# A two-layer decoder on one core: the low parts of unscaled weights are summed by an accumulating DMA in place of VectorE

## The chip, the cores and the metric

The kernel runs on 1 core of one Trainium2 chip. The metric is device microseconds of an execution. Three runs of the kernel before took 1812.57, 1816.09 and 1816.96 us; the median is 1816.09 us.

## The reference, cut to what matters

The input `x` is 512 tokens of 2048 values in float32. Two layers follow each other; each adds to the stream the normalised output of a mixer.

```
layer 0 (S5):   u, z = split(rmsnorm(h) @ w_in)          # 2048 x 4096
                y = gelu(state_space(u))                 # diagonal scan, 128 groups of 16 channels
                y = y * sigmoid(y @ w_glu + b_glu)       # 2048 x 2048
                h = h + rmsnorm((y * silu(z)) @ w_out)   # 2048 x 2048
shared:         k, v, f = split(rmsnorm(h) @ kv_w)       # 2048 x (2048 + 2048 + 16)
layer 1 (FoX):  q, z = split(rmsnorm(h) @ fox_w_in)      # 2048 x 4096
                o = causal attention of 16 heads with cumulative log forget gates
                h = h + rmsnorm((o * silu(z)) @ fox_w_out)
```

All products are wanted to about float32 precision.

## The kernel before

Every large product is made of three matmuls in the type float32r. Each operand is split into a high part, its copy in float32r, and a low part, the difference between the original and the high part. `mm3` (line 168) adds high times high, low weights times high, and high weights times low. So each piece of weights has a tile `whi` and a tile `wlo`, and both must be there before the matmuls on it can go on.

`piece` (line 138) prepares one piece, normally 128 partitions by 1024 elements (512 KB): it loads `wraw` from DRAM, multiplies it by a norm's scale where there is one, has ScalarE copy it to `whi` (through `act`, line 85), and has VectorE or GpSimd subtract to give `wlo` (line 152). `wraw` has four buffers, `whi` and `wlo` have two each. A column of 128 outputs needs two pieces; on each, TensorE runs 24 matmuls of 512 columns. `stream` and `ahead` keep one column prepared: after the matmuls of a column are issued in the program, the pieces of the next are asked for. The order of instructions on each engine is fixed when the program is built; the tile framework sets the semaphores.

The work runs in stages:

- Phase A: `w_in`, 32 columns (16 of `u`, 16 of `z`), with the state-space work between them: tables (`btps`), small kernels (`kps`), scans (`xps`) and outputs (`yps`), one of each for 16 steps. The first two columns are prepared by code of their own. The weights are unscaled. After the start, the queue that issues the weight loads (`self.weng`) is GpSimd's.
- Phase B: `w_glu`, 16 columns, unscaled, loads on GpSimd's queue.
- Phase C: `w_out`, by tokens (`tok_stage`, line 210), unscaled: 24 pieces of 512 output columns, then 8 of 256. The last two of these go to buffers of their own. Loads on SyncE's queue (SP), as in the stages that follow.
- Phase D: the columns of `k`, `q`, `v` and `z`, 128 pieces in all, each with a scale that GpSimd multiplies in (line 148), and the attention of 16 heads.
- Phase E: `fox_w_out`, as phase C.

Within `piece`, the instructions have a raised priority when `urgent` is set, so that they stand ahead of other work that is ready.

Of the kernel before, what the change touches and what calls it, by code (L numbers as in the profile page):

```python
# [12 lines left out]
F32R = mybir.dt.float32r  # L13
I32 = mybir.dt.int32
AF = mybir.ActivationFunctionType
ALU = mybir.AluOpType
# [49 lines left out]
class Kern:  # L66
# [72 lines left out]
    def piece(self, src, scale=None, pool=None, urgent=True, eng=None):  # L139

        nc = self.nc
        shp = list(src.shape)
        wp, n = pool or (self.wp, "")
        with self.tc.high_priority() if urgent else ExitStack():
            raw = self.wp.tile(shp, F32, tag="wraw", name="wraw", bufs=4)
            self.weng.dma_start(raw, src)
            if scale is not None:
                (eng or nc.vector).tensor_tensor(raw, raw, scale.unsqueeze(2).to_broadcast(shp), op=ALU.mult)  # L148
            hi = wp.tile(shp, F32R, tag=f"whi{n}", name="whi", bufs=2)
            lo = wp.tile(shp, F32R, tag=f"wlo{n}", name="wlo", bufs=2)  # L150
            self.act(hi, raw)
            (eng if eng and scale is None else nc.vector).tensor_tensor(lo, raw, hi, op=ALU.subtract)  # L152
        return hi, lo

    def stream(self, items, urgent=True):
# [975 lines left out]
```

## Time and profile before

| | |
|---|---|
| time of the three runs, median | 1816.09 us |
| the profiled execution: time | 1817.64 us |
| its span in the trace | 1815.9 us |
| mean granted clock of TensorE | 0.995 |
| TensorE matmul busy | 1786.6 us (98%) |
| VectorE busy | 1115.2 us (61%) |
| ScalarE busy | 614.4 us (34%) |
| GpSimd busy | 362.2 us (20%) |

The span is the stretch that the trace covers; the profiled execution's time lies 1.7 us above it. PE is TensorE's matmuls, PEld its weight loads, DVE VectorE, ACT ScalarE, POOL GpSimd, SP SyncE. Matmuls overlap in the engine, so a row that says 0.39 us for one does not mean that they follow each other at that distance; the starts tell that. Engine queues that only issue transfers have a q behind their name.

### The profile page before, as it was taken

Reading aid. Unit: us, or ns where it says so; the run is one execution under the profiler, and the core shown is the slowest. Engines: PE = TensorE matmul, PEld = TensorE weight load, DVE = VectorE, ACT = ScalarE, POOL = GpSimd, SP = SyncE. Lnnn points to the kernel's source line nnn. Section 1 sums busy time; section 2 is a strip of 40 time slices with the busy share of each in tenths; the row PEclk is TensorE's granted clock in tenths of the full one; section 3 lists DMA queues with packets and bytes.
Section 4 is the critical chain, followed back from the end, with each engine's and each line's share of the span. In section 5 each row is a group of like instructions: output and inputs, shape, how many; then the busy total and the mean of one; then the engine's idle time right before and its main releaser. Section 6 shows DMA issues by size and latency. Waiting matters only on the chain.

```text
span 1815.9 us, 26272 instructions
## 1 busy us (share of the span) xinstructions
PE 1786.6 (98%) x10518; PEld 1537.6 (85%) x10518; DVE 1115.2 (61%) x1629; ACT 614.4 (34%) x1032; POOL 362.2 (20%) x254
## 2 busy tenths in 40 slices
PE   9999999999999999999999999999999999999996
PEld 6888888888788888899889898989888898988886
DVE  9789999995855523256665655555555656542324
ACT  7334333333633322235223323222323332332222
POOL 1000000000000000033333433333333334300002
PEclk9999999999999999999999999999999999999998
DMA  9545555555544553343223323232232322344332
GB/s 326 144 137 157 146 149 147 145 147 168 186 146 153 165 186 93 94 134 128 82 88 93 94 89 94 86 99 87 88 99 87 97 90 88 93 134 162 93 95 103
DMA packets 141339, 226.57 MB, mean 125 GB/s; under 512 B 53601, under 2 KB 80497, under 8 KB 140961
## 3 DMA queue, kind: packets, MB, share of 16 engines
q1 hardware_dynamic: 126000, 173.79, 30.9%
q0 software_dynamic: 13056, 47.33, 8.7%
q10 hardware_dynamic: 2160, 3.77, 0.6%
q8 instruction: 82, 1.34, 0.3%
q14 instruction: 41, 0.33, 0.1%
HBM read 201.88 MB, written 22.97 MB: 124 GB/s over the span
## 4 chain that ended last, share of the span: by engine, by line
PE 90%; DVE 4%; DMA 2%; ACT 2%; SPq 1%; issue 1%; DVEq 0%; ACTq 0%
PE proj L171 18%; PE proj L173 18%; PE proj L172 17%; PE tok L232 6%; PE tok L233 6%; PE tok L231 6%; PE v L205 3%; PE v L206 3%; PE v L207 3%; PE yps L534 1%; DVE wlo L152 1%; PE t L940 1%; PE yps L539 1%; PE xps L506 1%; ACT ah L85 1%; PE btps L432 1%
## 5 line engine op out<-in xcount | busy, mean ns | idle before, releaser
L152 DVE TENSOR_TENSOR wlo<-wraw,whi 128x1024 fp32r<-128x1024 f32 x284 | 413.6, 1457 | 451.5 <-ACT whi L85 447.8
L85 ACT ACTIVATE whi<-wraw 128x1024 fp32r<-128x1024 f32 (+2 forms) x292 | 306.3, 1050 | 844.0 <-PE proj L173 518.5
L148 POOL TENSOR_TENSOR wraw<-wraw,vecs 128x1024 f32<-128x1024 f32 (+1 forms) x128 | 265.4, 2073 | 612.0 <-DMA wraw<-kv_k 281.5
L172 PE MATMUL proj<-BH,wlo 128*128 128x512 f32 (+1 forms) x816 | 308.9, 378 | 3.6 <-DVE wlo L152 3.6
L173 PE MATMUL proj<-BL,whi 128*128 128x512 f32 (+1 forms) x816 | 309.1, 379 | 1.9 <-DVE BL L73 1.9
L171 PE MATMUL proj<-BH,whi 128*128 128x512 f32 (+1 forms) x816 | 310.5, 380 | 0.0
L171 PE MATMUL proj<-ah,whi 128*128 128x512 f32 x768 | 302.5, 394 | 2.1 <-ACT zt L85 1.5
L173 PE MATMUL proj<-al,whi 128*128 128x512 f32 x768 | 300.3, 391 | 2.2 <-DVE al L73 1.7
L172 PE MATMUL proj<-ah,wlo 128*128 128x512 f32 x768 | 299.7, 390 | 0.2
L172 PEld LDWEIGHTS proj<-BH,wlo 128*128 128x128 f32 x816 | 154.6, 190 | 31.9 <-DVE wlo L152 4.1
L173 PEld LDWEIGHTS proj<-BL,whi 128*128 128x128 f32 x816 | 154.6, 189 | 30.7 <-DVE BL L73 2.3
L171 PEld LDWEIGHTS proj<-BH,whi 128*128 128x128 f32 x816 | 154.5, 189 | 27.8 <-ACT BH L85 0.2
L173 PEld LDWEIGHTS proj<-al,whi 128*128 128x128 f32 x768 | 144.1, 188 | 36.3 <-DVE al L73 6.3
L171 PEld LDWEIGHTS proj<-ah,whi 128*128 128x128 f32 x768 | 144.1, 188 | 33.6 <-ACT zt L85 1.9
L172 PEld LDWEIGHTS proj<-ah,wlo 128*128 128x128 f32 x768 | 144.2, 188 | 31.2 <-DVE wlo L152 1.3
L205 PE MATMUL v<-whi,BH 128*128 128x256 f32 (+1 forms) x512 | 145.6, 284 | 0.0
L206 PE MATMUL v<-wlo,BH 128*128 128x256 f32 (+1 forms) x512 | 145.2, 284 | 0.0
L207 PE MATMUL v<-whi,BL 128*128 128x256 f32 (+1 forms) x512 | 145.2, 284 | 0.0
L232 PE MATMUL tok<-wlo,BH 128*128 128x512 f32 (+1 forms) x320 | 111.0, 347 | 1.4 <-DVE wlo L152 1.4
L232 PE MATMUL tok<-wlo,ah 128*128 128x512 f32 (+1 forms) x320 | 111.0, 347 | 0.0
L231 PE MATMUL tok<-whi,BH 128*128 128x512 f32 (+1 forms) x320 | 110.9, 347 | 0.0
L233 PE MATMUL tok<-whi,al 128*128 128x512 f32 (+1 forms) x320 | 110.9, 347 | 0.0
(202 smaller groups left out, 2542.3 us busy)
## 6 DMA issues: line engine op xcount, KB each, us to landing
wraw<-w_fox SPq DMA_DIRECT2D x64, 512.0 KB
wraw<-w_in POOLq DMA_DIRECT2D x58, 512.0 KB, 4.4
wraw<-w_glu POOLq DMA_DIRECT2D x32, 512.0 KB, 4.3
wraw<-w_out SPq DMA_DIRECT2D x32, 512.0 KB
wraw<-kv_k SPq DMA_DIRECT2D x32, 512.0 KB
wraw<-w_fo SPq DMA_DIRECT2D x32, 512.0 KB
wraw<-kv_v SPq DMA_DIRECT2D x28, 512.0 KB
M<-kd SPq DMA_DIRECT2D x128, 64.0 KB
```

The source lines that it names most:

```text
L85: self.nc.scalar.activation(out, in_, f, **kw)
L148: (eng or nc.vector).tensor_tensor(raw, raw, scale.unsqueeze(2).to_broadcast(shp), op=ALU.mult)
L152: (eng if eng and scale is None else nc.vector).tensor_tensor(lo, raw, hi, op=ALU.subtract)
L171: mm(ps, lhsT=hi, rhs=xh, start=(k == 0), stop=False)
L172: mm(ps, lhsT=lo, rhs=xh, start=False, stop=False)
L173: mm(ps, lhsT=hi, rhs=xl, start=False, stop=(k == self.K - 1))
L205: nc.tensor.matmul(o, lhsT=xh[k][:, bs], rhs=hi, start=(k == 0), stop=False)
L206: nc.tensor.matmul(o, lhsT=xh[k][:, bs], rhs=lo, start=False, stop=False)
L207: nc.tensor.matmul(o, lhsT=xl[k][:, bs], rhs=hi, start=False, stop=(k == K - 1))
L231: nc.tensor.matmul(ps, lhsT=xh[k][:, bs], rhs=hi, start=(k == 0), stop=False)
L232: nc.tensor.matmul(ps, lhsT=xh[k][:, bs], rhs=lo, start=False, stop=False)
L233: nc.tensor.matmul(ps, lhsT=xl[k][:, bs], rhs=hi, start=False, stop=(k == K - 1))
```

## The change

For pieces without a scale, the subtraction is no longer made by VectorE or GpSimd. ScalarE writes the high part as before, then writes its negative into `wlo`; a transfer that GpSimd issues then adds `wraw` onto `wlo`, in SBUF. For pieces with a scale, the subtraction stays on VectorE.

```diff
             hi = wp.tile(shp, F32R, tag=f"whi{n}", name="whi", bufs=2)
-            lo = wp.tile(shp, F32R, tag=f"wlo{n}", name="wlo", bufs=2)
-            self.act(hi, raw)
-            (eng if eng and scale is None else nc.vector).tensor_tensor(lo, raw, hi, op=ALU.subtract)
+            if scale is None:
+
+                lo = wp.tile(shp, F32R, tag=f"wlo{n}", name="wlo", bufs=2)
+                self.act(hi, raw)
+                self.act(lo, hi, AF.Copy, scale=-1.0)
+                nc.gpsimd.dma_start(lo, raw, accum_op=ALU.add)
+            else:
+                lo = wp.tile(shp, F32R, tag=f"wlo{n}", name="wlo", bufs=2)
+                self.act(hi, raw)
+                nc.vector.tensor_tensor(lo, raw, hi, op=ALU.subtract)
         return hi, lo
```

## Rows read from the trace of the kernel before

**Rows 1.** Page, part 1: busy us, share of the span, instructions.

```profile
PE 1786.6 (98%) x10518; PEld 1537.6 (85%) x10518; DVE 1115.2 (61%) x1629; ACT 614.4 (34%) x1032; POOL 362.2 (20%) x254
```

**Rows 2.** Page, part 4: the chain that ended last, by engine.

```profile
PE 90%; DVE 4%; DMA 2%; ACT 2%; SPq 1%; issue 1%; DVEq 0%; ACTq 0%
```

**Rows 3.** TensorE's waits: waiter, awaited, us in total, times, longest us.

```profile
PE proj L172 <- DVE wlo L152: 3.6, 1, 3.6
...
PE tok L232 <- DVE wlo L152: 1.4, 1, 1.4
```

**Rows 4.** Timeline of ScalarE in phase C: start us, duration, what.

```profile
642.81 1.06 ACT L85 ACTIVATE whi<-wraw 128x1024 fp32r<-128x1024 f32 x1 [1.57 <-PE tok L233]
648.25 1.06 ACT L85 ACTIVATE whi<-wraw 128x1024 fp32r<-128x1024 f32 x1 [4.38 <-PE tok L233]
```

**Rows 5.** Timeline of VectorE in phase C.

```profile
643.90 1.22 DVE L152 TENSOR_TENSOR wlo<-wraw,whi 128x1024 fp32r<-128x1024 f32 x1 [1.94 <-ACT whi L85]
```

**Rows 6.** Timeline of phase B: two matmuls of TensorE, 24 apart.

```profile
599.72 0.39 PE L171 MATMUL proj<-ah,whi 128*128 128x512 f32 x1
...
605.16 0.39 PE L171 MATMUL proj<-ah,whi 128*128 128x512 f32 x1
```

**Rows 7.** DMA queues and issues (KB each, us to landing), and `wraw`'s landings.

```profile
q0 software_dynamic: 13056, 47.33, 8.7%
wraw<-w_in POOLq DMA_DIRECT2D x58, 512.0 KB, 4.4
wraw<-w_glu POOLq DMA_DIRECT2D x32, 512.0 KB, 4.3
mask<-c_mask POOLq DMA_DIRECT2D x1, 64.0 KB, 4.1
DMA to landing us min/median/max: 3.9/4.4/7.6
```

**Rows 8.** Timeline of VectorE and GpSimd in phase B.

```profile
504.24 1.22 DVE L152 TENSOR_TENSOR wlo<-wraw,whi 128x1024 fp32r<-128x1024 f32 x1
...
505.75 0.53 POOL L146 DMA_DIRECT2D wraw<-w_glu  x1 [6.68 <-DVE wlo L152]
```

**Rows 9.** The chain, in order of time: start us, us, what.

```profile
393.84 3.71 DMA y_d<-gy
```

**Rows 10.** The chain in phase A: state-space work between columns.

```profile
130.44 0.87 PE btps L432 x8
...
134.90 1.08 PE xps L506 x32
...
147.14 0.88 PE btps L432 x8
...
158.91 0.61 PE kps L472 x16
...
162.68 0.93 PE xps L506 x32
```

**Rows 11.** TensorE around one gap: timeline, then windows (PEclk is granted clock).

```profile
875.75 0.28 PE L171 MATMUL proj<-BH,whi 128*128 128x256 f32 x1
879.62 0.58 PE L172 MATMUL proj<-BH,wlo 128*128 128x256 f32 x1 [3.60 <-DVE wlo L152]
...
core 0: us, PE busy (x) PEld busy (x) DVE busy (x) ACT busy (x) POOL busy (x), PEclk, DMA share, GB/s
879.00:880.00 1.00, 0.38 (x1) 0.38 (x2) 1.00 (x2) 0.00 (x0) 0.00 (x0) 0.50 0.00 0
885.00:886.00 1.00, 1.00 (x9) 1.00 (x9) 0.00 (x0) 0.00 (x0) 0.24 (x1) 0.74 0.00 0
```

**Rows 12.** Windows inside phases A, B, C, E, columns as in rows 11.

```profile
100.00:400.00 300.00, 300.00 (x2387) 253.10 (x2389) 284.41 (x331) 112.33 (x192) 21.74 (x42) 1.00 0.54 147
430.00:635.00 205.00, 202.61 (x912) 164.45 (x911) 118.48 (x132) 84.02 (x104) 16.43 (x31) 1.00 0.53 168
640.00:800.00 160.00, 158.59 (x821) 136.40 (x820) 48.97 (x50) 41.91 (x65) 8.27 (x4) 1.00 0.38 120
1595.00:1795.00 200.00, 199.62 (x1097) 174.51 (x1096) 73.18 (x110) 55.98 (x92) 3.87 (x3) 1.00 0.36 114
```

## The prediction

> **What bounds the kernel now.** I read the page's busy shares and the chain first. TensorE (PE) is busy 98% of the span and carries 90% of the chain that ended last; VectorE carries 4% [rows 1, 2]. Then I asked what TensorE waits for: the longest single wait on a `wlo` of line 152 is 3.6 us, once, and it is on a scaled weight (the operand `BH` in `proj`), which the change does not touch; among unscaled weights it is 1.4 us, once [rows 3]. So the VectorE time that the change frees (156 subtractions of 1.22 us [rows 5], 190 us) comes from an engine that TensorE hardly waits for. At best it brings a microsecond or two. The question is whether the new path to `wlo` still meets its deadline.
>
> The deadline comes from the timeline. A piece of weights serves 24 matmuls, and TensorE takes 5.44 us over them (from 599.72 to 605.16 [rows 6]). `whi` and `wlo` have two buffers, so the copy to `whi` of a piece starts when TensorE leaves the piece two before it, and copies follow at the same 5.44 us [rows 4]. When the next copy starts, TensorE is already at this piece. A piece thus has 5.44 us from the start of its `whi` copy to the matmul that reads `wlo`, less some 0.2 us for the weight load ahead of it. Today the copy ends at 643.87 and VectorE's subtraction at 645.12 [rows 4, 5]: 2.3 us used, 2.9 to spare.
>
> **What the change removes, adds and moves.** There are 156 unscaled pieces: 60 of `w_in` (the first two columns do not pass through `piece`), 32 of `w_glu`, 32 each of `w_out` and `w_fo` (by the code: 24 full pieces and 8 of half width). The 128 scaled pieces keep their path, and I cost the whole attention stage at nothing.
>
> ScalarE: a second pass, taken as long as the `whi` copy, 1.06 us [rows 4]. 156 of them are 165 us on an engine busy 34% [rows 1]; as load it is hidden, but it stands in the piece's chain. In the first two stages it also holds back ScalarE's evacuations by 1 us; they feed work a column later, so nothing.
>
> GpSimd: one issue of 0.53 us, which starts 0.3 us after what it waits for (VectorE ends at 505.46, GpSimd issues at 505.75 [rows 8]). In the last two stages GpSimd's queue is otherwise nearly empty. In the first two it holds the weight loads too: the load four pieces on waits until this piece's accumulate has landed, and the next accumulate stands behind that load.
>
> The transfer: two ScalarE passes and GpSimd's wake take 2.1 + 0.3 us, so from issue to landing there is 5.44 - 0.2 - 2.4 = 2.85 us. No row shows an accumulating transfer, nor one from SBUF to SBUF. The nearest are these: 512 KB loads that GpSimd issues land after 4.4 us (median; 3.9 the fastest, 7.6 the slowest), a 64 KB one after 4.1 [rows 7], a 32 KB store from SBUF after 3.7 [rows 9]. Size matters little; none is under 2.85. A load holds each engine for 1.75 us: 8.7% of 1815.9 us is 158 us, for 47.33 MB, or 90 pieces [rows 7]. An accumulate must read its target besides its source, so I add one more stream: L = 4.4 + 1.75 = 6.15 us. Below, L = 3.9 (the second read costs nothing); above, 7.6 + 1.75 = 9.35.
>
> The Trainium skill's page "Collectives: The Full Stack" (section "The bandwidth ceiling: the fold count and why AG ≠ RS ≠ AR") also says that the add itself is free and the second source read halves the rate. No row here shows it. The page "DMA: Bandwidth & Descriptors" (section "Anatomy of one DMA — SWDGE (gpsimd) path") fits 2.0 us and bytes at 436 GB/s; for a plain load that is 3.2 us where the row has 4.4, and with two reads 4.4, an estimate that would give the second rival's time below.
>
> How the lateness adds up: with two buffers a late piece delays the start of the piece two later, but the piece between keeps its distance and is then on time. TensorE so idles once per column (two pieces), for d = L - 2.85 = 3.3 us.
>
> Stages of `w_out` and `w_fo`: 30 pieces each go through the two buffers (the last two have their own), 30 columns in all: 30 x 3.3 = 99 us.
>
> `w_glu`: 16 columns. A load is issued right ahead of the accumulate, so I add half of its 1.75 us: 16 x (3.3 + 0.9) = 67 us.
>
> `w_in`: 30 columns, with state-space work between some. The chain shows blocks of 4.7 to 5.5 us (130.44 to 135.98, 158.91 to 163.61) and single ones of 0.9 us (147.14) [rows 10]. With 16 steps there are 16 blocks of the first kind, 8 of the second, and 6 columns with none. A block hides as much of the gap as it is long: 16 x 0 + 8 x (4.2 - 0.9) + 6 x 4.2 = 52 us.
>
> Then the clock. In the one gap of 3.6 us (876.0 to 879.6) the granted clock fell to 0.50, the 1.2 GHz level, and stayed there until some 885.5 [rows 11]: half of 5.9 us, 2.9 us lost. Gaps of 4.2 us in the `w_glu` stage are longer than that one, those of 3.3 shorter. I charge half of the 16: 23 us. The Trainium skill's page "TensorE: Matmul & The Clock Gate" (section "HAM oscillation — how this bites in real kernels") warns of such repeated gaps; the row agrees, at one event.
>
> Sum: 99 + 67 + 52 + 23 = 241 us on the profiled execution's 1817.6, 2059; that execution is 1.5 us above the median of 1816.1, so **2057 us**.
>
> **The rivals.** First, a slower accumulate. If the engines need three streams for it (two reads and a write that do not overlap), L = 4.4 + 3.5 = 7.9, d = 5.05, and every gap is long enough for the clock: 30 x 7.95 + 16 x 8.85 + (8 x 7.95 + 6 x 8.85 + 16 x 0.9) = 512 us, 2328. For it speaks that the engines themselves fill up. They are busy 0.54 in the `w_in` stage and 0.53 with `w_glu` [rows 12]; 60 accumulates of 3.5 us in the 396 us from 21 to 417 add 0.53, 32 in 178 us add 0.63, so even two streams come over 1 at today's pace, and transfers will queue. Against it: the stalls stretch those stages, and the last two have room (0.38 and 0.36).
>
> Second, it lands about like a load, L = 4.4: d = 1.55, no clock loss: 30 x 1.55 + 16 x 2.45 + (8 x 1.55 + 6 x 2.45) = 113 us, 1929. With L = 3.9 and no queueing, d = 1.05: 32 + 17 + 8 = 57 us, 1873. For it speaks that landing time hardly depends on size in the rows; against it the second read, and the queueing.
>
> Third, the other side: not slower. If a transfer inside SBUF lands in under 2.85 us, no gap opens, and the 1.4 us wait goes: 1813 to 1817. It decides at L = 2.85. For it: no memory outside the core takes part. Against it: the store and the small loads take 3.7 and more, and have less to move. To gain over 0.3% (5.4 us) the freed VectorE would have to shorten the start or the joints between stages too; TensorE idles 1.4 us there on ScalarE's and VectorE's account in the third stage and 2.4 in the second [rows 12].
>
> **How the numbers follow.** Forecast (L from 5.3 to 7.6, which gives 30 x 2.45 + 16 x 3.35 + 40 = 168 us at one end, and some 400 with clock losses at the other: 1985 to 2220): 0.45. Slower accumulate, above 2220: 0.25. About like a load, 1870 to 1985: 0.20. Not slower: 0.10, of which faster 0.04. The 80% range runs from the fastest load without queueing, 1870, to L = 9.35 with the clock lost at every gap: 30 x 9.4 + 16 x 10.3 + (8 x 9.4 + 6 x 10.3 + 16 x 2.3) = 621 us, 2437. Some 0.1 lies on either side. The bound of 0.3% is about what a measurement of this kernel can tell from no change: the three times shown span 4.4 us.
>
> **What would show it.** In the profile after, VectorE loses line 152 for unscaled weights and ScalarE gains 156 passes of 1.06 us. Issues of accumulates should show a landing time near 6 us. TensorE's waits should be headed by transfers into `wlo`, once per column, 3 to 4 us each, in the stages of `w_glu`, `w_out` and `w_fo`, hardly after the long blocks of the `w_in` stage; the attention stage keeps its length. The forecast fails if landing is far from 6.15; if the gaps come at every piece (then the two buffers do not share the delay); if GpSimd's queue puts loads ahead so that accumulates wait on each other; or if gaps of 3.3 us already bring the clock down.

## The result and the profile after

| | before | after |
|---|---|---|
| median of the runs | 1816.53 us (1812.57 to 1817.81, 4 runs) | 2084.57 us (2080.11 to 2091.49, 4 runs) |
| ratio, 95% interval | | 1.1471 [1.1445, 1.1497] |
| profiled execution; its span | 1817.6; 1815.9 us | 2091.49; 2089.7 us |
| granted clock, mean of the span | 0.995 | 0.964 |

The changed kernel is 268 us slower; 241 us, a time of 2057 us, was forecast. The page of the kernel after answers to [rows 1, 2]: busy time by engine, then the chain that ended last by engine, then groups of instructions (busy, mean ns of one, idle before).

```profile
PE 1872.2 (90%) x10518; PEld 1571.0 (75%) x10518; DVE 934.6 (45%) x1473; ACT 769.0 (37%) x1188; POOL 498.1 (24%) x410
...
PE 54%; DMA 21%; issue 11%; DVE 7%; ACT 3%; SPq 2%; POOL 1%; POOLq 0%; DVEq 0%; ACTq 0%
...
L85 ACT ACTIVATE wlo<-whi 128x1024 fp32r<-128x1024 f32 x156 | 164.8, 1056 | 3.1
...
L155 POOL DMA_DIRECT2D wlo<-wraw x156 | 136.2, 873 | 507.2 <-ACT wlo L85 454.4
```

TensorE has fallen from 98% of the span to 90%, and transfers carry 21% of the chain. ScalarE's second pass costs the 1.06 us forecast, an accumulate's issue 0.87 us where a load's 0.53 was assumed. VectorE is busy 180.6 us less (1115.2 to 934.6), and nothing comes of it. TensorE's waits (total, times, longest) say for what:

```profile
PE proj L179 <- DMA wlo<-wraw: 115.5, 58, 5.1
PE tok L239 <- DMA wlo<-wraw: 72.5, 53, 10.7
PE yps L546 <- DMA M<-kd: 7.6, 4, 2.9
```

The wait on a scaled `wlo` that headed [rows 3] is gone from the head of the list; 111 waits on unscaled ones, 188.0 us, stand in its place.

To see where the time went I cut both traces at the same places of the work (the counts of matmuls agree within 1%): windows of the kernel after, with engines' busy time, granted clock, DMA share and GB/s, for the `w_in` stage (A), `w_glu` (B), `w_out` (C), attention (D) and `w_fo` (E). TensorE's busy time and length before were 454.80 of 460, 174.61 of 177, 180.59 of 182, 799.19 of 805 and 177.45 of 191 us.

```profile
0.00:561.00 561.00, 488.67 (x3238) 393.77 (x3239) 348.27 (x527) 251.84 (x386) 90.97 (x132) 0.95 0.80 200
561.00:814.00 253.00, 197.86 (x750) 150.14 (x749) 66.59 (x84) 94.79 (x114) 41.99 (x58) 0.93 0.68 169
814.00:1047.00 233.00, 193.06 (x990) 160.12 (x989) 26.95 (x62) 85.58 (x116) 41.50 (x40) 0.96 0.68 165
1047.00:1858.00 811.00, 801.44 (x4589) 708.69 (x4587) 465.94 (x732) 258.43 (x466) 287.06 (x144) 0.99 0.30 93
1858.00:2089.00 231.00, 191.13 (x957) 158.27 (x957) 26.88 (x69) 78.39 (x107) 36.55 (x37) 0.94 0.69 173
```

Each difference splits into more idle time of TensorE and more busy time over the same matmuls, which is mostly a lower clock (in A, 0.05 of 561 us is 28 of the 34; in B 0.07 of 253 is 18 of the 23):

| stage | longer by | idle | busy | forecast |
|---|---|---|---|---|
| A, `w_in` | 101 | 67 | 34 | 52 |
| B, `w_glu` | 76 | 53 | 23 | 67 + clock 23 |
| C, `w_out` | 51 | 38.5 | 12.5 | 49.5 |
| D, attention | 6 | 4 | 2 | 0 |
| E, `w_fo` | 40 | 26 | 14 | 49.5 |
| sum | 274 | 188 | 86 | 241 |

The 4 us of idle time in D are not the attention's: they are the wait for E's first `wlo` (4.35 us, until 1858.81), which lies just ahead of the cut.

Now the transfers. Queue 0 carries GpSimd's (packets, MB, share of 16 engines); under it the issues of the whole span (KB, us to landing).

```profile
q0 software_dynamic: 35520, 129.13, 28.7%
...
wlo<-wraw POOLq DMA_DIRECT2D x156, 512.0 KB, 6.1
...
wraw<-w_in POOLq DMA_DIRECT2D x58, 512.0 KB, 4.9
```

The median landing of 6.1 us is the forecast 6.15. By stretch it differs (115 to 500, in A; 570 to 810, in B; 818 to 1040, in C; E is as C):

```profile
wlo<-wraw POOLq DMA_DIRECT2D x44, 512.0 KB, 6.9
...
wlo<-wraw POOLq DMA_DIRECT2D x30, 512.0 KB, 6.6
...
wlo<-wraw POOLq DMA_DIRECT2D x31, 512.0 KB, 5.2
```

An accumulate holds each engine some 2.83 us: 28.7% of 2089.7 us less 158 us for the loads, over 156. This is an estimate, since it takes the loads at what they were before.

Last, the timeline of C in its steady part, which answers to [rows 4] (start, us; in brackets the idle time before and what ended it):

```profile
879.42 1.06 ACT L85 ACTIVATE whi<-wraw 128x1024 fp32r<-128x1024 f32 x1 [4.01 <-PE tok L240]
880.51 1.06 ACT L85 ACTIVATE wlo<-whi 128x1024 fp32r<-128x1024 f32 x1
885.54 1.06 ACT L85 ACTIVATE whi<-wraw 128x1024 fp32r<-128x1024 f32 x1 [3.97 <-PE tok L240]
...
892.29 1.06 ACT L85 ACTIVATE whi<-wraw 128x1024 fp32r<-128x1024 f32 x1 [4.61 <-PE tok L240]
...
881.86 0.86 POOL L155 DMA_DIRECT2D wlo<-wraw  x1 [5.29 <-ACT wlo L85]
...
886.97 0.50 PE L239 MATMUL tok<-wlo,BH 128*128 128x512 f32 x1 [1.01 <-DMA wlo<-wraw]
```

Follow the piece copied at 879.42: second pass at 880.51, issue at 881.86, first matmul on `wlo` at 886.97, 7.55 us after its start. The buffers it used are free when TensorE has done its 24 matmuls, and the copy two pieces on starts at 892.29: 12.87 us for two pieces, where before it was 2 x 5.44 = 10.88. So 2.0 us per column, and both of its pieces wait, not one of them. It is typical of the stage: from 834.82 to 976.58 22 copies to `whi` follow each other at 6.44 us on average, 12.89 for two.

### The profile page after: what moved, and what is told of

The parts are those of the page before. It is cut to its first block, busy times and chain, and to the rows that moved or that the text cites. A ratio compares the mean times of both kernels' runs of the same rounds, so it can differ in the third digit from the quotient of the medians.

```text
span 2089.7 us, 26569 instructions
## 1 busy us (share of the span) xinstructions
PE 1872.2 (90%) x10518; PEld 1571.0 (75%) x10518; DVE 934.6 (45%) x1473; ACT 769.0 (37%) x1188; POOL 498.1 (24%) x410
## 3 DMA queue, kind: packets, MB, share of 16 engines
q0 software_dynamic: 35520, 129.13, 28.7%
## 4 chain that ended last, share of the span: by engine, by line
PE 54%; DMA 21%; issue 11%; DVE 7%; ACT 3%; SPq 2%; POOL 1%; POOLq 0%; DVEq 0%; ACTq 0%
DMA wlo<-wraw 17%; PE proj L179 11%; PE proj L180 11%; PE proj L178 10%; PE tok L239 3%; PE v L212 3%; PE v L213 3%; PE v L214 3%; PE tok L240 3%; PE tok L238 2%; ACT wlo L85 1%; SPq L558 1%; PE t L947 1%; DMA y_d<-gy 1%; ACT whi L85 1%
## 5 line engine op out<-in xcount | busy, mean ns | idle before, releaser
L179 PE MATMUL proj<-ah,wlo 128*128 128x512 f32 x768 | 323.1, 421 | 115.6 <-DMA wlo<-wraw 115.5
L178 PE MATMUL proj<-ah,whi 128*128 128x512 f32 x768 | 317.0, 413 | 1.6 <-ACT whi L85 0.9
L180 PE MATMUL proj<-al,whi 128*128 128x512 f32 x768 | 315.3, 411 | 1.3 <-DVE al L73 0.9
L159 DVE TENSOR_TENSOR wlo<-wraw,whi 128x1024 fp32r<-128x1024 f32 (+1 forms) x128 | 221.4, 1729 | 183.8 <-ACT whi L85 183.7
L179 PEld LDWEIGHTS proj<-ah,wlo 128*128 128x128 f32 x768 | 153.6, 200 | 172.6 <-DMA wlo<-wraw 141.1
L155 POOL DMA_DIRECT2D wlo<-wraw x156 | 136.2, 873 | 507.2 <-ACT wlo L85 454.4
L178 PEld LDWEIGHTS proj<-ah,whi 128*128 128x128 f32 x768 | 153.1, 199 | 37.9 <-ACT whi L85 1.5
L180 PEld LDWEIGHTS proj<-al,whi 128*128 128x128 f32 x768 | 153.9, 200 | 35.3 <-DVE al L73 3.9
L180 PEld LDWEIGHTS proj<-BL,whi 128*128 128x128 f32 x816 | 155.0, 190 | 31.6 <-DVE BL L73 3.3
L85 ACT ACTIVATE wlo<-whi 128x1024 fp32r<-128x1024 f32 x156 | 164.8, 1056 | 3.1
L239 PE MATMUL tok<-wlo,BH 128*128 128x512 f32 (+1 forms) x320 | 116.4, 365 | 39.8 <-DMA wlo<-wraw 39.8
L239 PE MATMUL tok<-wlo,ah 128*128 128x512 f32 (+1 forms) x320 | 116.9, 366 | 32.7 <-DMA wlo<-wraw 32.7
```

The lines of the kernel that those rows point to most:

```text
L85: self.nc.scalar.activation(out, in_, f, **kw)
L155: nc.gpsimd.dma_start(lo, raw, accum_op=ALU.add)
L159: nc.vector.tensor_tensor(lo, raw, hi, op=ALU.subtract)
L178: mm(ps, lhsT=hi, rhs=xh, start=(k == 0), stop=False)
L179: mm(ps, lhsT=lo, rhs=xh, start=False, stop=False)
L180: mm(ps, lhsT=hi, rhs=xl, start=False, stop=(k == self.K - 1))
```

## The experiments

The first theory is the forecast's: two buffers, and a chain through a transfer that is longer than the time a piece gives. The rivals: the DMA engines are full, GpSimd's queue makes transfers wait on each other, or something else of the new path (ScalarE's pass, the copy itself) costs.

**Four pairs of buffers where C and E stream.** Alternate columns take the second pair of tags that the stage's end uses already.

```diff
-                    hi, lo = self.piece(src(k))
+                    hi, lo = self.piece(src(k), pool=(self.tp, "2") if k // kk % 4 > 1 else None)
```

> The changed kernel, but in the two stages by tokens the pieces rotate over four pairs of high and low tiles in place of two. Theory (a piece is late because its chain of two ScalarE passes, GpSimd's wake and a landing of 5.2 us, 7.5 us in all, starts only when TensorE frees a buffer 5.44 us before it is needed): with 16 us in hand no gap opens, the two stages lose the 91 us that they gained, 1990 to 2005 us in all. Rival (the engines' rate for accumulates is what sets the pace): the gaps stay, some 2084. Rival (the clock, brought down by gaps, is most of the 91): the same 1990 to 2005, so this run does not tell it from the theory; the windows of the changed kernel do.

Measured: 2015.18 us, 1.1096 [1.1077, 1.1114], 69 us less than the change. The timeline of ScalarE and the issues and window from 830 to 990:

```profile
872.32 1.06 ACT L85 ACTIVATE whi<-wraw 128x1024 fp32r<-128x1024 f32 x1 [2.85 <-PE tok L240]
...
877.76 1.06 ACT L85 ACTIVATE whi<-wraw 128x1024 fp32r<-128x1024 f32 x1 [3.29 <-PE tok L240]
```
```profile
wlo<-wraw POOLq DMA_DIRECT2D x27, 512.0 KB, 5.7
```
```profile
830.00:990.00 160.00, 155.66 (x792) 134.05 (x792) 9.89 (x16) 66.02 (x86) 26.99 (x29) 0.98 0.85 193
```

The pieces follow each other at 5.44 us again, although an accumulate lands no sooner (5.7) and the engines are busier (0.85). In these stages it is latency against the number of buffers. The median is 10 us above the upper end of what was expected: E, cut as above, is back to its old length, C stays 15 us longer. Half of that is one wait of 7.6 us at C's first pieces.

**B's loads on SyncE's queue**, so that no accumulate stands behind a load.

```diff
         self.phase_a(i)
+        self.weng = nc.sync
```

> The changed kernel, but the weight loads of the w_glu stage are issued by SyncE's queue, and only the accumulates by GpSimd's. Theory (in this stage GpSimd's queue is the pace: the next accumulate stands behind a load that waits until the accumulate before it has landed, 7.8 us per piece): the pace falls to that of the buffers, half of 2.4 + 6.6 + 5.2, 7.1 us per piece or less, 20 to 40 us gained, 2045 to 2065. Rival (the engines are full): transfers only queue elsewhere, 2080 to 2090.

Measured: 2085.68 us, 1.1477 [1.1453, 1.15]: no gain, and the theory failed. It is the rival's range, but its reason, full engines, does not hold, as a run with four pairs in B shows below. In B the pieces came 7.54 us apart (28 of them from 579.49 to 790.67) where they had been 7.92 (573.14 to 794.80). With the queue free, the buffers are the limit, almost as tight. B's gain of 12 us does not show in the whole time, as A was 7 us longer in the profiled execution.

**A plain copy in place of the accumulate.** It leaves the sum out.

```diff
-                nc.gpsimd.dma_start(lo, raw, accum_op=ALU.add)
+                nc.gpsimd.dma_start(lo, raw)
```

> The changed kernel with a plain copy of the raw weights onto the low part in place of the accumulate, so the sum is left out; the same bytes are written and the same waits are made. Theory (the second read costs some of the landing): the copy lands in about 4.4 us in the stages by tokens against 5.2, the gap per column falls by 0.8 there and by 1 to 2 us in the others, 2010 to 2045 us. Rival (the add costs nothing; the landing is the fixed cost of a transfer): 2075 to 2090.

Measured: 1938.76 us, 1.067 [1.0651, 1.0689], 146 us less than the change and 71 below the range expected. Its share of queue 0; the issues from 760 to 860, in C; and ScalarE there:

```profile
q0 software_dynamic: 35520, 129.13, 20.7%
```
```profile
wlo<-wraw POOLq DMA_DIRECT2D x18, 512.0 KB, 2.9
```
```profile
785.31 1.06 ACT L85 ACTIVATE whi<-wraw 128x1024 fp32r<-128x1024 f32 x1 [3.29 <-PE tok L240]
...
790.75 1.06 ACT L85 ACTIVATE whi<-wraw 128x1024 fp32r<-128x1024 f32 x1 [3.29 <-PE tok L240]
```

A copy inside SBUF lands in 2.9 us, not in a load's 4.4, and at 2.9 the pieces keep their 5.44 us, which agrees with the deadline of 2.85 us. The accumulate lands 2.3 us later than a copy in the same stage and holds an engine 2.83 us against 1.55 (20.7% of 1934.6 us, less 158, over 156, the same kind of estimate). What this kernel still loses is mostly in A (35 us to the last state-space output) and from there to C's first matmul (44), where the copies took 4.4 to 4.5 us.

**No transfer: VectorE adds the raw weight to the negative high part.**

```diff
-                nc.gpsimd.dma_start(lo, raw, accum_op=ALU.add)
+                nc.vector.tensor_tensor(lo, raw, lo, op=ALU.add)
```

> ScalarE writes the negative high part as in the changed kernel, but VectorE adds the raw weights onto it; no transfer. Theory (the transfer's landing is to blame, ScalarE's second pass of 1.06 us fits in the 2.9 us to spare): 1814 to 1822 us, same as before. Rival (the second pass costs by itself, as it stands ahead of ScalarE's evacuations in the busy first stage): 1830 to 1870.

Measured: 1825.03 us, 1.0043 [1.0028, 1.0058]. ScalarE's second pass by itself costs 8 us, most of it in A (the last state-space output at 441.2 instead of 435.0). That is 3 us above the theory's range and below the rival's. All the rest of the 268 us comes with the transfer: its issue, its landing and its bytes.

**Four pairs in B too**, with B's loads on SyncE's queue, and then with the loads left on GpSimd's. Both go together with the edit to C and E above.

```diff
+            self.nth = getattr(self, "nth", 0) + 1
+            pool = (self.tp, "2") if key[0] == "g" and hasattr(self, "tp") and self.nth % 2 else None
-            pcs = [self.piece(w[:, k:k + hk, :], None if scale is None else scale[:, k:k + hk], None, urgent, *eng)
+            pcs = [self.piece(w[:, k:k + hk, :], None if scale is None else scale[:, k:k + hk], pool, urgent, *eng)
...
+        self.weng = nc.sync
```

> The changed kernel with four pairs of high and low tiles in the w_glu stage and in the two stages by tokens, and the weight loads of the w_glu stage on SyncE's queue. Theory (the w_glu stage is held by two limits that lie close together, the buffers at half of 2.4 + 6.3 + 5.2 us and GpSimd's queue at landing + 0.6 us, so that taking one away alone brought some 10 us): with both gone that stage falls from 94 us over the kernel before to 0 to 20, some 1930 to 1950 us in all. Rival (its engines are full: 0.53 busy before, and 32 accumulates of 2.83 us in 177 us add 0.51): it stays 30 us or more over, 1955 to 1990.

> As the run before it, but the weight loads of the w_glu stage stay on GpSimd's queue, where each waits for the landing of an accumulate and the next accumulate stands behind it. Theory (GpSimd's queue alone holds the stage at some 7.2 us per piece against 5.44): 1985 to 2005 us, little better than four pairs in the stages by tokens alone (2015). Rival (buffers alone set that stage): 1930 to 1950, as with SyncE's queue.

Measured: 1951.34 us, 1.074 [1.0714, 1.0765], with SyncE's queue, 1 us above what its theory gave; 1991.51 us, 1.0965 [1.0935, 1.0996], without, as its theory expected. From the last state-space output to the first matmul of C that reads `wlo` it is 228.8 us with both, 274.4 with the buffers alone, 284.2 with the queue alone (the run above), 296.1 in the change, and 202.3 before. Taken away singly, the limits of the buffers and of the queue give 22 and 12 us; both together give 67. Of the kernel with both, here are the windows before and from 600:

```profile
517.00:600.00 83.00, 61.46 (x232) 45.27 (x229) 30.13 (x32) 45.15 (x50) 9.69 (x12) 0.93 0.87 227
600.00:745.00 145.00, 145.00 (x637) 119.91 (x636) 49.22 (x64) 72.56 (x89) 21.52 (x25) 0.99 0.95 235
```

From 600 on TensorE is never idle, with the engines busy 0.95, and the pieces follow at 5.44 us. So the engines did not hold B. By sum they should be just full: before, they were busy 0.50 of B's 177 us, 88 us, and 32 accumulates of 2.83 us add 91. What is left over the kernel before, 26 us, lies where A passes into B: there TensorE is idle 21.5 of 83 us, and the clock is 0.93. Its waits there are for `wlo` and for ScalarE; what makes them was not followed up.

**The accumulate in two halves**, so that the first sets out before ScalarE has finished.

```diff
-                self.act(lo, hi, AF.Copy, scale=-1.0)
-                nc.gpsimd.dma_start(lo, raw, accum_op=ALU.add)
+                for q in range(2):
+                    s = slice(q * shp[1] // 2, (q + 1) * shp[1] // 2)
+                    self.act(lo[:, s], hi[:, s], AF.Copy, scale=-1.0)
+                    nc.gpsimd.dma_start(lo[:, s], raw[:, s], accum_op=ALU.add)
```

> The changed kernel, but the negative copy and the accumulate are made in two halves, each half as large. Theory (the landing has a part that goes with size; a plain copy of the whole landed in 2.9 us in the w_out stage, the accumulate in 5.2): a half lands in some 4 us and is issued 0.5 us sooner, and TensorE can begin on it; the gaps in the stages by tokens shrink from 2.0 to below 1 us a column, 2000 to 2060 us. Rival (landing is fixed, or TensorE waits for both halves; GpSimd issues twice, 0.87 us each): 2085 to 2140.

Measured: 2092.87 us, 1.1534 [1.1489, 1.158]: no gain, as the rival said. In C a half landed after 5.5 us, a whole after 5.2, and GpSimd issued twice. Two halves in flight together land no sooner than the whole.

**A third pair of buffers in A**, with the loads on GpSimd's queue and then on SyncE's. The room comes from the raw tiles, three instead of four. What that costs by itself no run shows.

```diff
+        if pool is None and getattr(self, "in_a", False):
+            self.na = getattr(self, "na", -1) + 1
+            pool = (self.sp, "3") if self.na % 3 == 2 else None
-            raw = self.wp.tile(shp, F32, tag="wraw", name="wraw", bufs=4)
+            raw = self.wp.tile(shp, F32, tag="wraw", name="wraw", bufs=3)
...
-            self.weng = nc.gpsimd
```

(The last line is taken out in the second of the two.)

> The changed kernel with a third pair of high and low tiles in the w_in stage, and three raw buffers in place of four everywhere (for the room). Theory (there GpSimd's queue holds the pace: 6.9 us of landing and 0.6 us for the load between, 7.5 us per piece, where TensorE's own pace with the state-space work is 7.4): it gains 0 to 25 us, 2060 to 2085. Rival (buffers set the pace there too): 50 us or more, below 2035.

> The changed kernel with a third pair of tiles in the w_in stage (and three raw buffers), and the weight loads of that stage on SyncE's queue. Theory (with three pairs GpSimd issued load and accumulate back to back, 8.1 us per piece, of which 7.4 landing: its queue held the pace): two accumulates can now be under way at once, and the stage gains 30 to 80 us, 2000 to 2050. Rival (the transfer engines, 0.80 busy there, or SyncE's queue, which issues the state-space work's small transfers, set the pace): 2065 to 2110.

Measured: 2079.8 us, 1.1456 [1.1422, 1.1491], and 2079.38 us, 1.1445 [1.1421, 1.1469]. The first went as expected. The timeline of GpSimd in it, in A:

```profile
216.44 0.55 POOL L149 DMA_DIRECT2D wraw<-w_in  x1 [7.01 <-DMA wlo<-wraw]
216.98 0.90 POOL L158 DMA_DIRECT2D wlo<-wraw  x1
224.03 0.55 POOL L149 DMA_DIRECT2D wraw<-w_in  x1 [6.16 <-DMA wlo<-wraw]
224.58 0.90 POOL L158 DMA_DIRECT2D wlo<-wraw  x1
```

A load waits until an accumulate has landed, and the next accumulate stands right behind that load: one at a time, some 8 us for each piece. The second took the loads off that queue, and gained nothing, against the 30 to 80 us expected. TensorE's waits for `wlo` in A fell from 51.4 us (up to the last output, in the change) to 4.8, but two others took their place. One runs through the stage (here from 100 to 480), the other is a single wait near the start, shown with SyncE's queue ahead of it:

```profile
PE yps L549 <- DMA M<-kd: 31.6, 22, 4.6
```
```profile
55.52 0.33 SPq L149 DMA_DIRECT2D wraw<-w_in  x1
55.95 0.94 SPq L703 DMA_DIRECT2D xtok<-x  x2
...
62.22 0.79 PE L181 MATMUL proj<-ah,whi 128*128 128x512 f32 x1 [12.80 <-ACT zt L85]
```

The single wait comes from SyncE's queue: a weight load, held until an accumulate had landed, stood ahead of the last loads of `x`, and ScalarE worked on these before it came to `zt`. With the loads on GpSimd's queue this wait was 3.2 us. It is read from the timeline; no run put the loads of `x` ahead.

`M` comes by transfers of 64 KB on SyncE's queue, which the accumulates do not touch. Either that queue, which now carries the weight loads too, or the engines must be late. With the loads still on GpSimd's queue the wait for `M` was 21.0 us, so SyncE's queue is not needed for most of it.

**The same, with A's accumulates over a quarter of each piece.** It keeps the queues and the issues, and takes away bytes only.

```diff
+                q = slice(0, shp[1] // 4 if getattr(self, "in_a", False) else shp[1])
-                nc.gpsimd.dma_start(lo, raw, accum_op=ALU.add)
+                nc.gpsimd.dma_start(lo[:, q], raw[:, q], accum_op=ALU.add)
```

> The kernel with three pairs and SyncE's loads in the w_in stage, but there each accumulate covers only the first quarter of the piece, so three quarters of the low parts stay without the raw weights (the sum is incomplete); issues and waits are as many as before, the bytes of the accumulates a quarter. Theory (what held that stage at 2079 us in all was the transfer engines, 0.79 busy, on which the state-space work's small transfers wait): the stage gets 50 to 80 us shorter, 2000 to 2030 us. Rival (SyncE's queue, which has the loads between the state-space work's issues): 2060 to 2085.

Measured: 2022.82 us, 1.1138 [1.111, 1.1167]. The waits and the window of A, then the window of the kernel with whole accumulates:

```profile
PE yps L550 <- DMA M<-kd: 5.2, 6, 1.6
```
```profile
115.00:460.00 345.00, 336.59 (x2633) 281.22 (x2632) 263.71 (x319) 163.86 (x253) 38.71 (x45) 0.99 0.63 156
```
```profile
115.00:480.00 365.00, 330.38 (x2477) 273.98 (x2473) 254.34 (x305) 156.33 (x240) 36.13 (x42) 0.94 0.79 186
```

The last state-space output came at 462.4 us instead of 520.9. With the loads where they were, the wait for `M` fell from 31.6 to 5.2 us, and the clock rose from 0.94 to 0.99. So the bytes of the accumulates, on engines busy 0.79, made the transfers of `M` late. A quarter also lands sooner (3.1 us against 6.1), but `wlo` was waited for only 4.8 us in A before. SyncE's queue keeps its part at the start: the wait for `zt` is still there, 14.5 us.

**All remedies together**, and **VectorE's subtraction back in A alone**, with the four pairs and SyncE's loads in the later stages.

```diff
-            if scale is None:
+            if scale is None and not getattr(self, "in_a", False):
```

> All the remedies at once: three pairs in the w_in stage, four in the three others, all weight loads on SyncE's queue, three raw buffers. If GpSimd's queue held the w_in stage, it is 30 to 80 us below the kernel with the remedies in the later stages alone (1951): 1870 to 1920. If the engines or SyncE's queue did: 1940 to 1980. In no case below the kernel before, whose TensorE was busy 98%.

> The kernel with the remedies in the later stages, and the w_in stage with VectorE's subtraction as before the change. If the stages add up (the w_in stage lost 83 us up to its last output, some 90 with its tail): 1855 to 1875 us. Rival (a part of that loss only moved there from the stages after it): above 1890.

Measured: 1945.13 us, 1.072 [1.0704, 1.0736], and 1847.29 us, 1.0178 [1.0163, 1.0193]. The first is what was expected if the engines or SyncE's queue held A. The remedies for A add no clear gain to those for the other stages (1951.34 us; the intervals of the ratios overlap), and the wait for `zt` is there again, 14.2 us. The second is 8 us below the range expected: the stages add up, and a little more than that comes back. With A as it was, its last output is back at 434.6 us (435.0 before), and the kernel is 104 us faster than with accumulates there and all else equal. It is still 33 us slower than the kernel before: 20 of them lie between that output and C's first matmul on `wlo`, and again ahead of B's steady part, since from 512 to 656 TensorE is not idle. No version beat the kernel before, where TensorE is busy 98% [rows 1].

## Why the prediction was right, and where it was not

**The chain and its deadline: right.** TensorE now waits for transfers into `wlo`, as said. The deadline of 2.85 us from issue to landing fits the runs, which show it between two values only: at 2.9 us (the copy) pieces follow at 5.44 us, at 5.2 they don't, and more buffers restore 5.44 at 5.7. No stage became shorter by VectorE's freed time, and the attention stage kept its length within 6 us.

**The landing time: right by luck, as errors cancelled.** 6.15 us was a load's 4.4 and one more stream of 1.75; measured 6.1. The parts were off: a copy inside SBUF lands in 2.9 us undisturbed, the add costs 2.3 more, and 1.4 to 1.7 more come on top in A and B, where the engines and GpSimd's queue carry more. The row for SBUF transfers was taken from loads and small stores [rows 7, 9], and neither was near. So the third rival's premise ("no memory outside the core takes part") was true of a copy. It is the accumulate that misses the deadline. The Trainium skill's page "Collectives: The Full Stack" (section "The bandwidth ceiling: the fold count and why AG ≠ RS ≠ AR") has the rule that the second read halves the rate. These runs agree: 2.83 us of an engine against 1.55, a factor of 1.8. The fit on the Trainium skill's page "DMA: Bandwidth & Descriptors" (section "Anatomy of one DMA — SWDGE (gpsimd) path") gives 3.2 us for one stream (measured 2.9) and gave 4.4 as an estimate for two (measured 5.2 undisturbed).

**Stages of `w_out` and `w_fo`: 99 us forecast, 91 measured, made up of other things.** Its step "TensorE so idles once per column" failed: nearly every piece waits, 0.3 to 2.5 us each. The prediction had named that as a sign of failure. The sum per column survives, since a piece's chain and its 24 matmuls alternate on each buffer whichever piece shows the wait: 2 x 5.44 + (5.06 - 2.85) = 13.1 us by its formula, 12.87 measured. With some 2.0 us in place of 3.3, 30 columns make 60 us, not 99. That 91 came out near 99 is in part luck again.

The rest are long waits that the term did not hold, and the lower clock behind them: 4.0 and 4.5 us in E, and three at the two ends of C. C has 39.8 us of waits, of which 15.0 are spread over 19 waits from 870 to 1000; one at its first pieces is 7.2 us, and two at its end are 3.0 and 10.7. For this last one, here are ScalarE, GpSimd and TensorE of the kernel after:

```profile
1005.34 1.06 ACT L85 ACTIVATE wlo<-whi 128x1024 fp32r<-128x1024 f32 x1
...
1010.31 1.89 POOL L148 TENSOR_TENSOR wraw<-wraw,vecs 128x1024 f32<-128x1024 f32 x1 [5.74 <-DMA wraw<-kv_k]
1014.06 1.89 POOL L148 TENSOR_TENSOR wraw<-wraw,vecs 128x1024 f32<-128x1024 f32 x1 [1.86 <-DMA wraw<-kv_k]
1017.12 2.00 POOL L148 TENSOR_TENSOR wraw<-wraw,vecs 128x1088 f32<-128x1088 f32 x1 [1.17 <-DMA wraw<-kv_vf]
1019.07 0.87 POOL L155 DMA_DIRECT2D wlo<-wraw  x1
...
1023.66 0.58 PE L239 MATMUL tok<-wlo,BH 128*128 128x256 f32 x1 [10.66 <-DMA wlo<-wraw]
```

ScalarE is done at 1006.4, but the accumulate goes out at 1019.07: three scalings of the next stage's weights stand ahead of it on GpSimd, waiting for their loads. "GpSimd's queue is otherwise nearly empty" was true of the stage and false at its end. The kernel with plain copies has the same wait, 9.9 us. It is read from the timeline; no run moved these scalings.

**`w_glu`: 67 and 23 for the clock forecast, 53 and 23 measured.** The charge for the queue was of the right kind: a load goes out when an accumulate lands, the next accumulate right behind it. It was the smaller half of the story. Queue and buffers are two limits of nearly one size: 7.7 us for a piece with the queue alone (17 pieces from 642.78 to 773.23 of the kernel with four pairs and GpSimd's loads), 7.5 with the buffers alone.

**`w_in`: 52 us forecast, 101 measured. This is the term that failed.** The step that "a block hides as much of the gap as it is long" took the pace as given by buffers, with the state-space work as cover. TensorE waited 62.7 us for `wlo` there. The queue makes accumulates go one at a time, some 8 us for a piece. With a third pair and the queue relieved, the waits for `wlo` are nearly gone, but those for `M` rise from 7.6 us to 39.2 over the stage, because the bytes of the accumulates make its transfers late. And the clock, charged only in B, cost here too: most of 34 us of longer busy time. How much of A's 101 us belongs to the queue and how much to the bytes in the changed kernel itself stays open, since relieving the one brought out the other, and moving the loads cost 12.8 us at the start.

The first rival had named the engines, at 3.5 us for an accumulate instead of 2.83. It was right that transfers get in each other's way in A (0.80 busy). Its premise that a sum over 1 sets the pace did not hold in B: there the sum is 179 us for 177, and TensorE kept its pace all the same once buffers and queue were relieved.

**The clock: 23 us forecast, 66 to 86 measured.** The prediction had one event to go by, a gap of 3.6 us [rows 11]. It charged gaps longer than that, in B alone, and said that gaps of 3.3 us bringing the clock down would be a failure. Shorter gaps did so, but not each time. Two of B's, and the windows after them:

```profile
645.70 0.50 PE L179 MATMUL proj<-ah,wlo 128*128 128x512 f32 x1 [2.81 <-DMA wlo<-wraw]
...
661.23 0.50 PE L179 MATMUL proj<-ah,wlo 128*128 128x512 f32 x1 [2.22 <-DMA wlo<-wraw]
...
646.00:650.00 4.00, 4.00 (x19) 3.26 (x18) 0.00 (x0) 0.00 (x0) 1.38 (x2) 1.00 0.68 155
662.00:663.00 1.00, 1.00 (x4) 0.80 (x3) 0.00 (x0) 0.00 (x0) 0.91 (x2) 0.50 0.36 37
...
665.00:666.00 1.00, 1.00 (x5) 0.78 (x5) 0.00 (x0) 0.00 (x0) 0.00 (x0) 0.91 1.15 279
...
887.00:892.00 5.00, 5.00 (x22) 4.15 (x23) 0.00 (x0) 0.69 (x1) 0.86 (x1) 1.00 0.80 190
```

After 2.81 us of idle time the clock is at 1.00; after 2.22 us it is at 0.50, the 1.2 GHz level, until some 665. Of B's 22 gaps of 0.9 us and more, 10 have the 0.50 behind them, and between 1.86 and 2.83 us there are 7 with it and 5 without. So the length of a single gap does not decide it, and no run here shows what does. After the gap of 1.0 us in C the clock stayed at 1.00. The 86 us are the growth of busy time over all stages. By the granted clock over the span it is 66: 0.036 of 2089.7 us, less 0.005 of 1815.9. The rest was not followed up; the first record behind a gap reads 0.50 us where others read 0.39. The Trainium skill's page "TensorE: Matmul & The Clock Gate" (section "HAM oscillation — how this bites in real kernels") warns of repeated gaps; by these runs that warning was worth more than the 23 us charged.

**ScalarE's pass: "nothing" forecast, 8 us measured** with no transfer in the way.

## What to carry to other kernels

Before work moves from an idle engine to a transfer, count its latency against the time that the buffers leave (here 5.2 us against 2.85). Then ask which other transfers its bytes will make late: engines busy 0.95 did not hold up a stage with enough buffers, while at 0.79 a stage that waits for small transfers lost time to them. Cures act on one limit at a time, and where two limits lie close, each cure alone gives little (22 and 12 us) and both together much (67). A cure can also bring out a limit of its own, as the loads on SyncE's queue did (12.8 us). Look also at what else stands on the queue that issues the transfer, to the end of the stage, since an issue waits behind whatever was put ahead of it.

## What was not expected of the hardware

A 512 KB copy inside SBUF landed after 2.9 us, sooner than a load of the same size (4.4 us) or a 32 KB store from SBUF (3.7 us). An accumulate of 512 KB took 5.2 us, and one of 256 KB, two in flight, 5.5. GpSimd took 0.87 us to issue an accumulate and 0.53 to issue a copy of the same tile. In B of the kernel after, seven pauses of TensorE of 1.86 to 2.82 us had the 1.2 GHz level behind them, and five of 2.38 to 2.83 us had not. With the engines busy 0.95, TensorE went 145 us without a pause, although an accumulate then landed after 6.5 us (median).
